# Two token tiles per weight tile: interleaving gate, up, query and value products in two PSUM banks

## Chip, cores, metric

One core of a Trainium2 chip runs the whole program in one launch. The metric is the device time of one execution in microseconds; the time of a kernel is the median of its runs.

## What is computed

A sequence of 256 tokens of width 1024 goes through one mixed block (RWKV-7 time mixing and differential attention side by side, a squared-ReLU feed-forward of width 4096, a gated per-layer embedding), a final norm, and two layers of a second block (SwiGLU feed-forward of width 2816, attention, SwiGLU again). Everything is fp32. The parts that the change touches:

```python
x = x + jnp.square(jax.nn.relu(rmsnorm(x, norm_mlp_g) @ w_ff1)) @ w_ff2
gate = jax.nn.sigmoid(rmsnorm(x, norm_ple_g) @ w_ple_gate)
x = x + (p @ w_ple) * gate
x = rmsnorm(x, final_norm_g)
for layer in range(2):
    x = x + 0.5 * swiglu(rms_norm(x, norm_ffn1), ffn1_w_gate, ffn1_w_up, ffn1_w_down)
    xn = rms_norm(x, norm_mix)
    mixed = (mix_stick_moba, mix_forget_dilated)[layer](xn, w_in, ...)
    x = x + mixed @ w_out
    x = x + 0.5 * swiglu(rms_norm(x, norm_ffn2), ffn2_w_gate, ffn2_w_up, ffn2_w_down)
```

where `swiglu(x, g, u, d) = (silu(x @ g) * (x @ u)) @ d`.

## The kernel before

The 256 tokens are two token tiles t0 and t1 of 128 rows. The residual `x` stays on the chip; the weights (some 252 MB) are streamed through it once. Each weight unit is 128 x 1024 fp32 (512 KB): SP issues its DMA into one of three `raw` buffers (L341), ACT copies it to a rounded `hi` (L365), DVE subtracts to get `lo` (L366), and eleven hi/lo buffers hold the units that TensorE still needs. A product is three matmuls for each row tile of 128 input features (`mm3`): hi weights by hi activations, lo by hi, hi by lo. The weights are the moving operand (128x512), the transposed activations `hT` (for gate, up, queries, values, output) or `aT` (for down) the stationary one. A product of one token tile and 512 output columns is 8 row tiles, 24 matmuls, in one of eight PSUM banks.

The order of TensorE's instructions is written by the program itself, by a planner (`Weave`) that keeps a model time. After each `mm3` it lets side streams run whose due time has passed: the flips (four transposes, an ACT copy `aTh` or `hTh`, a DVE subtraction `aTl` or `hTl`), the attention's own work. The order on the other engines comes from a scheduler. All engines take their instructions in order, so what is listed behind a waiting instruction waits too.

A feed-forward (`mlp`) goes by chunks of 512 (one of 256) hidden columns. For a chunk it takes gate and up for both token tiles (FF1 has one product in place of two). ACT evacuates the first product with the token's norm factor `hT[t].r` (L463), DVE multiplies in the second (L465); this `a` is then flipped. The down product of a chunk (`down`) runs after gate and up of the following chunk; after the last chunk the down products of the last two chunks come in one go, t0 then t1. Its first four row tiles (12 matmuls) need the flip of the chunk before, the next four that of the last chunk.

Order of a chunk before: in the first chunk t0 gate, t0 up, t1 gate, t1 up; later gate t0, gate t1, up t0, up t1. Each is 24 matmuls in a row in one bank.

Attention (`attn_layer`) takes four groups of heads in the order 2, 0, 3, 1; queries and keys of a group are one product of 512 columns, values one of 256 (264 for one of layer 1). Each query product goes to a side stream that normalises, applies rope (L546 to L565; POOL makes one part in the buffer `rb`, of which there is one) and flips. At the end `out` multiplies by `w_out`; its first six row tiles come before the last head group is ready, the last two after. It adds the result to `x` (L876), and the next norm's half begins (`Normed.half`: `h` on DVE L909, a square on ACT L413, a flip). A norm's second half needs the flip of that half only from row tile 4 of the next product on.

`Ple` computes the gated embedding: the gate of t0 (both column halves), the values of t0, the values of t1, the gate of t1.

## Time and profile before

| | |
|---|---|
| median of 3 runs | 1530.09 us (1528.64 to 1535.28) |
| the profiled execution | 1529.78 us |
| its span | 1528.0 us |
| TensorE (PE) busy | 1489.4 us, 97% |
| VectorE (DVE) busy | 927.9 us, 61% |
| ScalarE (ACT) busy | 760.8 us, 50% |
| mean DMA rate | 167 GB/s |

Rough stages: mixed block to 250 us, FF1 to 469, embedding gate to 499, first FFN of layer 0 to 690, attention to 820, second FFN to 1010, and the same three of layer 1 to 1204, 1336 and 1528. A duration of a matmul in the profile overlaps with the next one's; the distance between two starts is what one costs.

### The profile page before, as it was taken

What the parts mean: (1) busy time and instruction counts of PE and PEld (TensorE: products, weight loads), DVE (VectorE), ACT (ScalarE), POOL (GpSimd) and SP (SyncE); (2) the same over time, 40 slices, a digit from 0 to 9 for tenths busy, and PEclk for the clock granted to TensorE, in tenths of its full rate; (3) what the DMA queues carried; (4) which work ended last, traced back from release to release, by engine and by line L of the source; (5) the groups of instructions that cost most, each with busy time, mean ns of one, the idle gap of its engine ahead of it and who ended that gap; (6) DMA issues with size and microseconds to landing.
All of it is one profiled execution on the core that took longest, in us unless ns stands there. A gap on an engine that the chain in (4) does not pass through costs nothing.

```text
span 1528.0 us, 22440 instructions
## 1 busy us (share of the span) xinstructions
PE 1489.4 (97%) x8804; PEld 1237.2 (81%) x8804; DVE 927.9 (61%) x1528; ACT 760.8 (50%) x1142; POOL 46.7 (3%) x70
## 2 busy tenths in 40 slices
PE   7999989999999999999999999999999999999999
PEld 6887767788888788887888888887888888888887
DVE  5886777755558755557546554566545787565552
ACT  6644445644536544447565444445444566464441
POOL 1120100000000000001100000000000010000000
PEclk9999999999999999999999999999999999999999
DMA  7233238655544765536434665547555444275551
GB/s 253 90 118 107 98 119 278 202 194 177 182 151 157 223 200 190 185 132 193 138 111 147 198 194 192 179 156 220 190 189 182 141 154 136 78 227 180 179 182 53
DMA packets 76298, 254.97 MB, mean 167 GB/s; under 512 B 11040, under 2 KB 13344, under 8 KB 76192
## 3 DMA queue, kind: packets, MB, share of 16 engines
q1 hardware_dynamic: 76192, 253.53, 51.1%
q8 instruction: 69, 1.13, 0.3%
q14 instruction: 37, 0.30, 0.1%
HBM read 252.45 MB, written 1.05 MB: 166 GB/s over the span
## 4 chain that ended last, share of the span: by engine, by line
PE 81%; DVE 7%; DMA 5%; ACT 4%; issue 2%; POOL 0%; SPq 0%; ACTq 0%; DVEq 0%; POOLq 0%
PE b L279 77%; DMA raw<-in_w_dram 4%; PE b L283 4%; DVE lo L366 2%; ACT hi L365 2%; DMA grow<-in_norm_mix_g_dram 0%; DMA stage<-in_consts_dram 0%; DMA lam<-in_lam_k_dram 0%; POOL rb L563 0%; POOL rb L562 0%; DVE hTl L366 0%; DVE c L1132 0%; DVE U L1260 0%; DVE u L1129 0%; ACT e L376 0%
## 5 line engine op out<-in xcount | busy, mean ns | idle before, releaser
L366 DVE TENSOR_TENSOR lo<-raw,hi 128x1024 fp32r<-128x1024 f32 (+1 forms) x465 | 561.9, 1214 | 356.1 <-ACT hi L365 350.1
L365 ACT ACTIVATE hi<-raw 128x1024 fp32r<-128x1024 f32 (+1 forms) x465 | 485.6, 1050 | 417.4 <-PE b L279 207.6
L279 PE MATMUL b<-hi,hTh 128*128 128x512 f32 (+2 forms) x1312 | 499.9, 381 | 0.7 <-ACT hi L365 0.7
L279 PE MATMUL b<-hi,hTl 128*128 128x512 f32 (+2 forms) x1312 | 489.9, 373 | 0.5 <-DVE hTl L366 0.5
L279 PE MATMUL b<-lo,hTh 128*128 128x512 f32 (+2 forms) x1312 | 489.7, 373 | 0.8 <-DVE lo L366 0.8
L279 PEld LDWEIGHTS b<-hi,hTl 128*128 128x128 f32 x1312 | 247.4, 189 | 47.8 <-DVE hTl L366 0.9
L279 PEld LDWEIGHTS b<-hi,hTh 128*128 128x128 f32 x1312 | 247.6, 189 | 46.1 <-issue 2.5
L279 PEld LDWEIGHTS b<-lo,hTh 128*128 128x128 f32 x1312 | 247.8, 189 | 44.2 <-DVE lo L366 1.5
L279 PE MATMUL b<-hi,aTh 128*128 128x512 f32 x480 | 191.6, 399 | 0.0
L279 PE MATMUL b<-hi,aTl 128*128 128x512 f32 x480 | 188.1, 392 | 0.0
L279 PE MATMUL b<-lo,aTh 128*128 128x512 f32 x480 | 187.4, 390 | 0.0
L279 PEld LDWEIGHTS b<-hi,aTl 128*128 128x128 f32 x480 | 90.1, 188 | 20.1
L279 PEld LDWEIGHTS b<-lo,aTh 128*128 128x128 f32 x480 | 90.3, 188 | 18.0
L279 PEld LDWEIGHTS b<-hi,aTh 128*128 128x128 f32 x480 | 90.2, 188 | 17.6
L463 ACT ACTIVATE a<-b,rsi_x 128x512 f32<-128x512 f32 (+1 forms) x52 | 34.4, 662 | 55.3 <-PE b L279 55.2
L365 ACT ACTIVATE aTh<-b 128x512 fp32r<-128x512 f32 (+1 forms) x64 | 36.3, 567 | 43.2 <-PE b L283 41.8
L465 DVE SCALAR_TENSOR_TENSOR a<-b,rsi_x,a 128x512 f32<-128x512 f32 (+1 forms) x52 | 37.2, 716 | 32.1 <-PE b L279 17.3
L366 DVE TENSOR_TENSOR aTl<-b,aTh 128x512 fp32r<-128x512 f32 (+1 forms) x64 | 41.8, 653 | 20.0 <-ACT aTh L365 19.7
L279 PE MATMUL b<-hi,hT1h 128*128 128x512 f32 (+1 forms) x128 | 53.4, 418 | 0.0
L279 PE MATMUL b<-lo,hT1h 128*128 128x512 f32 (+1 forms) x128 | 47.8, 373 | 0.6 <-DVE lo L366 0.6
L279 PE MATMUL b<-hi,hT1l 128*128 128x512 f32 (+1 forms) x128 | 47.4, 371 | 0.0
L365 ACT ACTIVATE hTh<-b 128x512 fp32r<-128x512 f32 (+1 forms) x48 | 25.2, 541 | 38.1 <-PE b L283 33.5
(582 smaller groups left out, 1293.6 us busy)
## 6 DMA issues: line engine op xcount, KB each, us to landing
raw<-in_w_dram SPq DMA_DIRECT2D x446, 512.0 KB, 4.2
raw<-in_w_dram SPq DMA_DIRECT2D x16, 384.0 KB, 3.4
grow<-in_norm_ffn_dram SPq DMA_DIRECT2D x4, 512.0 KB, 5.3
x<-in_x_dram SPq DMA_DIRECT2D x4, 256.0 KB, 6.2
x<-in_x_dram SPq DMA_DIRECT2D x2, 512.0 KB, 4.4
grow<-in_norm_mix_dram SPq DMA_DIRECT2D x2, 512.0 KB, 4.8
out_dram<-x SPq DMA_DIRECT2D x4, 256.0 KB, 2.0
raw<-in_w_dram SPq DMA_DIRECT2D x2, 396.0 KB, 3.6
```

What stands on the lines that cost most here:

```text
L279: self.nc.tensor.matmul(out=out, lhsT=lhsT, rhs=rhs, start=start, stop=stop, skip_group_check=skip)
L283: self.nc.tensor.transpose(out=out, in_=src, identity=self.ident)
L365: self.nc.scalar.activation(out=hi, in_=src, func=AF.Copy)
L366: self.nc.vector.tensor_tensor(out=lo, in0=src, in1=hi.bitcast(F32), op=ALU.subtract)
L463: nc.scalar.activation(out=a[t], in_=p, func=AF.Silu if kind == "swiglu" else AF.Relu, scale=hT[t].r)
L465: nc.vector.scalar_tensor_tensor(out=a[t], in0=p, scalar=hT[t].r, in1=a[t], op0=ALU.mult, op1=ALU.mult)
```

## The change

`both` takes a list of weight blocks and, for each, runs both token tiles side by side: for row tile k the three matmuls of t0 into one bank, then the three of t1 into another. Gate and up of each chunk, the values and the queries use it. With `apart` (the first chunk's first product, the first query product) t0 and t1 still run one after the other. In the first chunk the order is then gate t0, gate t1, up of both.

`out` takes both column halves side by side for the first six row tiles, t0 then t1, all before the last head group is waited for, and then the last two row tiles half by half.

In `Ple` the gate's weights come as two blocks of 512 columns, with the value weights between them; the values are copied out of PSUM by ACT (into `pw`, now two buffers), and the products run in the order gate(t0, half 0), values(t0), gate(t1, half 0), gate(t0, half 1), values(t1), gate(t1, half 1).

The number of matmuls, transposes, weight bytes and DMAs is unchanged.

```diff
@@ -451,13 +451,9 @@
         for ci, w in enumerate(chunks):
             kt = w // 128
             ws = [self.wblock((n, i, ci)) for n in names[:-1]]
-            order = [(t, j) for t in range(2) for j in range(nw)] if ci == 0 else [(t, j) for j in range(nw) for t in range(2)]
             a, aT = {}, {}
-            for t, j in order:
-                b = self.bank()
+            for t, j, b in self.both(hT, ws, w, ci == 0):
                 p = b[1][:, :w]
-                for k in range(8):
-                    self.mm3(p, hT[t].at(k), ws[j][k], k == 0, k == 7)
                 if j == 0:
                     a[t] = pool.tile([128, 512], F32, tag="a", name="a", bufs=4)[:, :w]
                     nc.scalar.activation(out=a[t], in_=p, func=AF.Silu if kind == "swiglu" else AF.Relu, scale=hT[t].r)
@@ -474,6 +470,17 @@
                 held = held[1:]
         for t in range(2):
             self.down(acc, t, held, res, after)
+
+    def both(self, hT, ws, n, apart=False):
+
+        for j, w in enumerate(ws):
+            for ts in ((0,), (1,)) if apart and j == 0 else ((0, 1),):
+                bs = [self.bank() for _ in ts]
+                for k in range(8):
+                    for t, b in zip(ts, bs):
+                        self.mm3(b[1][:, :n], hT[t].at(k), w[k], k == 0, k == 7)
+                for t, b in zip(ts, bs):
+                    yield t, j, b
 
     def down(self, acc, t, held, res, after=None):
         fresh = (t, 0) not in acc
@@ -795,10 +802,7 @@
             w = self.wblock((win, 0, ("v", g)))
             n = w[0][0].shape[1]
             vt, bs = [], []
-            for t in range(2):
-                b = self.bank()
-                for k in range(8):
-                    self.mm3(b[1][:, :n], hT[t].at(k), w[k], k == 0, k == 7)
+            for t, _, b in self.both(hT, [w], n):
                 v = pool.tile([128, 256], F32, name="v", tag="v", bufs=5)
                 nc.scalar.activation(out=v, in_=b[1][:, :256], func=AF.Copy, scale=hT[t].r)
                 vt.append(v)
@@ -819,10 +823,7 @@
             else:
                 qkT = [pool.tile([128, 4, 256], F32, name="qkT", tag="qkT", bufs=4)]
             ready = []
-            for t in range(2):
-                b = self.bank()
-                for k in range(8):
-                    self.mm3(b[1], hT[t].at(k), w[k], k == 0, k == 7)
+            for t, _, b in self.both(hT, [w], 512, i == 0):
                 self.held -= 1
                 ready.append(W.spawn(self.qk_side(pool, kind, g, t, b, hT[t], qkT)))
             if i < 3:
@@ -865,29 +866,30 @@
                 self.split(oTs[t][0][:, c], oTs[t][1][:, c], oT[:, c, t * 128:t * 128 + 128])
         acc = {}
 
-        def out(t, s, ks):
-            c = slice(s * 512, s * 512 + 512)
-            if (t, s) not in acc:
-                acc[t, s] = self.bank()
-            p = acc[t, s][1]
+        def out(t, halves, ks):
+            for s in halves:
+                if (t, s) not in acc:
+                    acc[t, s] = self.bank()
             for k in ks:
-                self.mm3(p, (oTs[t][0][:, k], oTs[t][1][:, k]), (wo[k][0][:, c], wo[k][1][:, c]), k == 0, k == 7)
-            if 7 in ks:
+                for s in halves:
+                    c = slice(s * 512, s * 512 + 512)
+                    self.mm3(acc[t, s][1], (oTs[t][0][:, k], oTs[t][1][:, k]), (wo[k][0][:, c], wo[k][1][:, c]), k == 0, k == 7)
+            for s in halves if 7 in ks else ():
+                c = slice(s * 512, s * 512 + 512)
+                p = acc[t, s][1]
                 nc.vector.tensor_tensor(out=self.x[t][:, c], in0=self.x[t][:, c], in1=p, op=ALU.add)
                 self.drop(acc[t, s], 1.0)
                 after(t, s)
 
         first, rest = range(6), range(6, 8)
-        out(0, 0, first)
-        out(0, 1, first)
-        out(1, 0, first)
+        out(0, (0, 1), first)
+        out(1, (0, 1), first)
         W.need(sides[3][0])
-        out(0, 0, rest)
-        out(0, 1, rest)
-        out(1, 1, first)
+        out(0, (0,), rest)
+        out(0, (1,), rest)
         W.need(sides[3][1])
-        out(1, 0, rest)
-        out(1, 1, rest)
+        out(1, (0,), rest)
+        out(1, (1,), rest)
 
 
 GROUPS = (2, 0, 3, 1)
@@ -1041,8 +1043,9 @@
 
 def first_plan():
     out = ffn_plan(("w_ff1", "w_ff2"), 0, FF1_CHUNKS)
-    out.append((("w_ple_gate", 0, 0), (0, D), [(0, D)]))
+    out.append((("w_ple_gate", 0, 0), (0, D), [(0, 512)]))
     out.append((("w_ple", 0, 0), (0, 256), [(0, D)]))
+    out.append((("w_ple_gate", 0, 1), (0, D), [(512, D)]))
     return out
 
 
@@ -1699,42 +1702,53 @@
             lo = pool.tile([128, 2, 128], F32R, name="pTl", tag="pTl", bufs=2)
             self.flips.append(K.flip_side(pt, hi, lo, 4.0))
 
-    def product(self, lhs, w, evacuate):
+    def product(self, lhs, w):
         K = self.K
-        for s in range(2):
-            c = slice(s * 512, s * 512 + 512)
-            b = K.bank()
-            n = len(w)
-            for k in range(n):
-                K.mm3(b[1], lhs(k), (w[k][0][:, c], w[k][1][:, c]), k == 0, k == n - 1)
-            evacuate(s, c, b[1])
-            K.drop(b)
+        b = K.bank()
+        for k in range(len(w)):
+            K.mm3(b[1], lhs(k), w[k], k == 0, k == len(w) - 1)
+        return b
 
     def run(self, pool, hT, after):
         K, nc = self.K, self.K.nc
         K.quota = 4
-        wg = K.wblock(("w_ple_gate", 0, 0))
-        wp = K.wblock(("w_ple", 0, 0))
         gt = [pool.tile([128, D], F32, name="pg", tag="pg", bufs=2) for _ in range(2)]
-        pw = pool.tile([128, D], F32, name="pw", tag="pw", bufs=1)
-
-        def gate(t):
-            self.product(hT[t].at, wg, lambda s, c, p: nc.scalar.activation(out=gt[t][:, c], in_=p, func=AF.Sigmoid, scale=hT[t].r))
-
-        def value(t, evacuate):
+        pw = [pool.tile([128, D], F32, name="pw", tag="pw", bufs=2) for _ in range(2)]
+        half = lambda s: slice(s * 512, s * 512 + 512)
+
+        def gate(t, s, wg):
+            b = self.product(hT[t].at, wg)
+            nc.scalar.activation(out=gt[t][:, half(s)], in_=b[1], func=AF.Sigmoid, scale=hT[t].r)
+            K.drop(b)
+
+        def value(t, s, wp):
             f = K.W.need(self.flips[t])
-            self.product(lambda k: (f[0][:, k], f[1][:, k]), wp, evacuate)
-
-        def merge(t, s, c, v):
-            nc.vector.tensor_tensor(out=gt[t][:, c], in0=gt[t][:, c], in1=v, op=ALU.mult)
+            c = half(s)
+            b = self.product(lambda k: (f[0][:, k], f[1][:, k]), [(h[:, c], l[:, c]) for h, l in wp])
+            nc.scalar.activation(out=pw[t][:, c], in_=b[1], func=AF.Copy)
+            K.drop(b)
+
+        def merge(t, s):
+            c = half(s)
+            nc.vector.tensor_tensor(out=gt[t][:, c], in0=gt[t][:, c], in1=pw[t][:, c], op=ALU.mult)
             nc.vector.tensor_tensor(out=K.x[t][:, c], in0=K.x[t][:, c], in1=gt[t][:, c], op=ALU.add)
             after(t, s)
 
-        gate(0)
-        value(0, lambda s, c, p: merge(0, s, c, p))
-        value(1, lambda s, c, p: nc.scalar.activation(out=pw[:, c], in_=p, func=AF.Copy))
-        self.product(hT[1].at, wg, lambda s, c, p: (
-            nc.scalar.activation(out=gt[1][:, c], in_=p, func=AF.Sigmoid, scale=hT[1].r), merge(1, s, c, pw[:, c])))
+        w = K.wblock(("w_ple_gate", 0, 0))
+        wp = K.wblock(("w_ple", 0, 0))
+        gate(0, 0, w)
+        for s in range(2):
+            value(0, s, wp)
+        merge(0, 0)
+        gate(1, 0, w)
+        w = K.wblock(("w_ple_gate", 0, 1))
+        gate(0, 1, w)
+        merge(0, 1)
+        for s in range(2):
+            value(1, s, wp)
+        merge(1, 0)
+        gate(1, 1, w)
+        merge(1, 1)
 
 
 class FinalNorm(Normed):
```

Three places show how TensorE's order moves (names: `a` the hidden activations of a token tile, `aTh`/`aTl` its flip, `hi`/`lo` weights, `b` a PSUM bank, `h` the scaled input of the next norm; x4 stands for four transposes of one half).

TensorE, last chunk of FF1, before: the transposes of t0's `a` come inside t1's product, those of t1's inside the down product.

```order
L283 MATMUL b_4594<-ident_83,a_4573 128x128 x4
...
L279 MATMUL b_3615<-hi_4465,aTl_4407 128x512
L279 MATMUL b_3615<-hi_4617,aTh_4576 128x512
L279 MATMUL b_3615<-lo_4618,aTh_4576 128x512
L279 MATMUL b_3615<-hi_4617,aTl_4577 128x512
L283 MATMUL b_4654<-ident_83,a_4610 128x128 x4
```

The change, the same place:

```order
L279 MATMUL b_3608<-hi_4458,aTl_4432 128x512
L283 MATMUL b_4644<-ident_83,a_4598 128x128 x4
L283 MATMUL b_4651<-ident_83,a_4603 128x128 x4
L279 MATMUL b_3608<-hi_4610,aTh_4601 128x512
L279 MATMUL b_3608<-lo_4611,aTh_4601 128x512
L279 MATMUL b_3608<-hi_4610,aTl_4602 128x512
```

The 21 matmuls between t0's transposes and the first matmul that reads `aTh` of the last chunk are gone; both tiles' transposes stand right ahead of it. The same is found at the last chunk of all five feed-forwards.

TensorE, end of attention of layer 0 and first gate product of the next FFN, before: t0's `h` (h_7881) is flipped inside the last `out` products, t1's (h_7950) inside t0's gate product, which opens with b_8032.

```order
L283 MATMUL b_7918<-ident_83,h_7881 128x128 x4
...
L283 MATMUL b_7931<-ident_83,h_7881 128x128 x4
...
L279 MATMUL b_7908<-hi_7761,hTl_7768 128x512
L279 MATMUL b_8032<-hi_7986,hTh_7879 128x512
...
L279 MATMUL b_8032<-hi_7992,hTl_7880 128x512
L283 MATMUL b_8042<-ident_83,h_7950 128x128 x4
...
L283 MATMUL b_8055<-ident_83,h_7950 128x128 x4
```

The change, the same place; t0's `h` is h_7903, t1's h_7939, the gate product opens with b_8028:

```order
L283 MATMUL b_7946<-ident_83,h_7903 128x128 x4
...
L279 MATMUL b_7857<-hi_7772,hTl_7779 128x512
L279 MATMUL b_8028<-hi_7982,hTh_7901 128x512
...
L279 MATMUL b_8028<-hi_7982,hTl_7902 128x512
L283 MATMUL b_8032<-ident_83,h_7903 128x128 x4
L283 MATMUL b_8039<-ident_83,h_7939 128x128 x4
...
L279 MATMUL b_8028<-hi_7982,hTl_7902 128x512
L283 MATMUL b_8049<-ident_83,h_7939 128x128 x4
```

Before, 21 matmuls stand between the transposes of t0's first half and the gate's first matmul, and t1's come 9 and 15 matmuls into the gate. Now 3 matmuls stand there, and t0's second half and both halves of t1 are transposed within the gate's first 6 matmuls. Attention of layer 1 ends alike.

TensorE, start of FFN1 of layer 0, before: t0's `a` (a_5266) is flipped 15 matmuls into t1's gate, after gate and up of t0 (48 matmuls).

```order
L279 MATMUL b_5296<-hi_5200,hTh_5060 128x512
L279 MATMUL b_5296<-lo_5201,hTh_5060 128x512
L279 MATMUL b_5296<-hi_5200,hTl_5061 128x512
L283 MATMUL b_5312<-ident_83,a_5266 128x128 x4
L279 MATMUL b_5296<-hi_5200,hTh_5060 128x512
```

The change; t0's `a` is a_5269, t1's a_5296:

```order
L279 MATMUL b_5426<-lo_5387,hTh_4906 128x512
L279 MATMUL b_5426<-hi_5386,hTl_4907 128x512
L283 MATMUL b_5443<-ident_83,a_5269 128x128 x4
L283 MATMUL b_5450<-ident_83,a_5296 128x128 x4
L279 MATMUL b_5427<-hi_5386,hTh_5056 128x512
```

The two flips now come together, 15 matmuls into the second chunk's gate, after gate and up of both tiles (96 matmuls).

## Rows read from the trace of the kernel before

**Rows 1.** The page, busy time by engine: busy us, share of the span, instructions.
```profile
PE 1489.4 (97%) x8804; PEld 1237.2 (81%) x8804; DVE 927.9 (61%) x1528; ACT 760.8 (50%) x1142; POOL 46.7 (3%) x70
```

**Rows 2.** The waits of PE, 240 to 1528 us: engine, line, releaser, total, times, longest.
```profile
PE b L283 <- DVE a L465: 2.7, 3, 2.3
```

**Rows 3.** PE timeline, a gate product: start, duration, engine, line, operation, tiles, idle and releaser.
```profile
407.76 0.40 PE L279 MATMUL b<-hi,hTh 128*128 128x512 f32 x1
...
411.95 0.39 PE L279 MATMUL b<-hi,hTh 128*128 128x512 f32 x1
```

**Rows 4.** PE timeline, a down product, banks alternating every three matmuls.
```profile
425.04 0.39 PE L279 MATMUL b<-hi,aTl 128*128 128x512 f32 x1
...
430.03 0.39 PE L279 MATMUL b<-hi,aTh 128*128 128x512 f32 x1
```

**Rows 5.** Windows: busy us and count by engine, then PEclk, DMA share, GB/s.
```profile
514.40:517.60 3.20, 3.20 (x10) 2.48 (x9) 2.91 (x4) 2.43 (x4) 0.00 (x0) 0.54 0.48 164
905.50:912.50 7.00, 7.00 (x33) 5.75 (x31) 3.12 (x3) 2.62 (x3) 0.00 (x0) 1.00 0.33 114
```

**Rows 6.** PE timeline, start of FFN1 of layer 0.
```profile
510.69 0.40 PE L279 MATMUL b<-hi,hTl 128*128 128x512 f32 x1
513.43 0.66 PE L283 MATMUL b<-ident,a 128*128 128x128 f32 x4 [2.33 <-DVE a L465]
...
514.61 0.59 PE L279 MATMUL b<-hi,hTh 128*128 128x512 f32 x1
...
517.99 0.43 PE L279 MATMUL b<-hi,hTl 128*128 128x512 f32 x1
```

**Rows 7.** PE timeline, second chunk of FFN1 of layer 1.
```profile
1038.43 0.40 PE L279 MATMUL b<-hi,hTl 128*128 128x512 f32 x1
...
1040.74 0.51 PE L279 MATMUL b<-lo,hTh 128*128 128x512 f32 x1 [0.76 <-DVE lo L366]
```

**Rows 8.** PE timeline, attention of layer 0, fourth pair of query products.
```profile
746.45 0.39 PE L279 MATMUL b<-hi,hTl 128*128 128x512 f32 x1
747.84 0.63 PE L283 MATMUL b<-ident,w__7155 128*128 128x128 f32 x4 [1.01 <-DVE w__7155 L565]
```

**Rows 9.** Timeline of all engines, one transposed `a` with nothing in its way.
```profile
1505.22 0.60 PE L283 MATMUL b<-ident,a 128*128 128x128 f32 x4
...
1505.58 0.48 PE L279 MATMUL b<-hi,aTh 128*128 128x512 f32 x1
...
1505.86 0.60 ACT L365 ACTIVATE aTh<-b 128x512 fp32r<-128x512 f32 x1 [5.36 <-PE b L283]
...
1506.49 0.69 DVE L366 TENSOR_TENSOR aTl<-b,aTh 128x512 fp32r<-128x512 f32 x1 [3.74 <-ACT aTh L365]
```

**Rows 10.** The same chain with a weight split ahead on ACT and DVE.
```profile
1183.29 0.60 PE L283 MATMUL b<-ident,a 128*128 128x128 f32 x4
1183.44 1.06 ACT L365 ACTIVATE hi<-raw 128x1024 fp32r<-128x1024 f32 x1 [3.79 <-DMA raw<-in_w_dram]
...
1184.54 1.23 DVE L366 TENSOR_TENSOR lo<-raw,hi 128x1024 fp32r<-128x1024 f32 x1 [2.96 <-ACT hi L365]
...
1185.68 0.68 DVE L366 TENSOR_TENSOR aTl<-b,aTh 128x512 fp32r<-128x512 f32 x1
```

**Rows 11.** Timeline, end of attention of layer 0: DVE and ACT.
```profile
819.89 0.68 DVE L876 TENSOR_TENSOR x<-x,b 128x512 f32<-128x512 f32 x1
...
822.57 0.61 ACT L413 ACTIVATE junk<-x 128x512 f32<-128x512 f32 x1
```

**Rows 12.** ACT timeline, rope of layer 0: the square that opens the chain.
```profile
739.57 0.58 ACT L546 ACTIVATE sq<-b 128x512 f32<-128x512 f32 x1
```

**Rows 13.** POOL timeline, the same chain.
```profile
744.12 1.18 POOL L562 TENSOR_TENSOR rb<-qn,gs 128x256 f32<-128x256 f32 x1 [30.69 <-DVE qn L553]
745.25 1.72 POOL L563 TENSOR_TENSOR rb<-qn,gs 128x256 f32<-128x256 f32 x1
```

**Rows 14.** DVE timeline, the same chain: its end.
```profile
747.00 0.69 DVE L565 TENSOR_TENSOR w__7155<-w__7155,rb 128x512 f32<-128x512 f32 x1 [0.63 <-POOL rb L563]
```

## The prediction

> **What bounds the kernel.** I read the page first: TensorE is busy 97% of the span, no other engine over 61% [rows 1]. Its queue bounds the kernel, so nothing on ACT, DVE or the DMA queues counts before TensorE waits for it. The numbers of matmuls, transposes and weight bytes don't change, so the time can move in three ways only: the distance between two matmuls, TensorE's waits, and its clock. So I next read the waits of PE after 240 us (the mixed block ahead keeps its code) [rows 2], the distances in the PE timelines, and the granted clock.
>
> Distances: 18 steps of a gate product take 411.95 - 407.76 = 4.19 us, 0.233 each [rows 3]; 22 steps of a down product, which alternates between two banks every three matmuls, 430.03 - 425.04 = 4.99, 0.227 each [rows 4]. The granted clock is 1.00 in long matmul runs, which is 2.4 GHz, and 0.54 after the longest wait, near 1.2 GHz [rows 5].
>
> **What it removes.** The waits of before that the new order touches:
>
> 1. Start of FFN1, layer 0. 510.69 to 513.43 is 2.74 us where one step was due: 2.5 lost waiting for t0's `a`, which needs the norm factor of the final norm. Then the clock is down: 514.61 to 517.99 holds 8 steps in 3.38 us, where 8 x 0.233 = 1.86 were due, so 1.5 more [rows 6]. The order now flips `a` after 96 + 15 matmuls in place of 48 + 15, that is 48 x 0.233 = 11 us later; the factor was 2.5 us late. **-4.0**, nothing of it left.
> 2. FFN1, layer 1, second chunk: 1038.43 to 1040.74 is 2.31 us for 2 steps, 1.85 lost on late weights (hi, then lo) [rows 7]. In the first chunk the gate's buffers now come free during t1's gate, 24 matmuls (5.6 us) earlier, and the up weights row by row. **-1.85** (0 if the DMA, not a buffer, was late).
> 3. Attention of layer 0: 746.45 to 747.84, 1.16 lost on the rope of t0's last query product [rows 8]. With both tiles side by side the flip stands about 53 matmuls (12.3 us) behind the pair's end, and the chain takes 8.1 us (below). **-1.16**.
>
> Sum -7.0 us.
>
> **What it adds.** A flip is a chain over three engines. Free of other work: transposes at 1505.22, `aTh` from 1505.86 for 0.60, `aTl` from 1506.49 for 0.69, so 1.96 us until all is there; TensorE itself spends 0.36 on four transposes (1505.22 to the next matmul 1505.58) [rows 9]. With a weight split ahead, 1.06 on ACT and 1.23 on DVE: 1183.29 to 1186.36, 3.07 us [rows 10]. Before, 21 or more matmuls (4.9 us) covered it.
>
> 4. Last chunk of each of five feed-forwards: t0's transposes, t1's, then at once the matmul that reads t0's `aTh`. It could start 0.72 us after the first transposes and gets `aTh` at 1.24: 0.5 lost; the third matmul needs `aTl` at 1.96 where 1.24 + 2 x 0.23 = 1.70 was due: 0.26. So 0.8 each, and 0.8 + 3.07 - 1.96 = 1.9 with a split ahead [rows 9, 10]. FF1's order has two hi copies right ahead of `aTh` and two lo subtractions ahead of `aTl`: 1.7. The last FFN has no weights left: 0.8. The other three, in whose order a single split stands between: 1.0 each, near the free end, since that split has mostly run when the transposes come. **+5.5** (4.0 to 8.4).
> 5. End of both attentions. Set 0 at the end of `out`'s last matmul. t0's first `x` half is final 18 matmuls and four transposes earlier, 18 x 0.233 + 0.36: -4.55. DVE then goes `x` 0.68, lo 1.23, `h`, `x`, `x`, `h` (as large as the first, 0.68 each) [rows 10, 11] to +0.1, a further `h` to 0.8, t1's second `x` to 1.6, lo 1.2 to 2.8, and only then `hTl` of t0's first half, till about 3.6. ACT has, from the second `x` at -1.3, a square 0.6 with its readout 0.2, a hi copy 1.06, t1's square 0.8, then `hTh` 0.6: 2.0. The gate's first matmul was due at 0.2 and starts at about 2.0: 1.8 lost; its third was due at 2.5 and gets `hTl` at about 3.65: 1.15 lost. t0's halves had 21 matmuls of cover before, now 3. **+2.9 per layer, +5.8**. Low end 1.4 per layer (the split of 1.06 to 1.23 not in the way); high end 4.4, with the 1.5 us of clock that the wait of [rows 6] was followed by.
> 6. Rope in attention of layer 1. The chain in layer 0: square at 739.57, rope's end at 747.00 + 0.69, 8.1 us [rows 12, 14]; t1 has to wait for `rb`, which one tile holds from 744.12 to 746.97, 2.9 us [rows 13]. With both tiles ready together t1's is done near 10.5 to 11. In layer 1 the order puts t1's flip about 36 matmuls, 8.5 us, behind the pair. **+2.0** (0 to 3.0).
>
> Within a feed-forward's other chunks the flips stand 15 matmuls (3.5 us) behind the pair, and the second `a` is ready 0.7 later than the first: near 2 us after the pair's end. Nothing. The `Ple` change has the same matmuls; DVE's added halves hide behind 24 matmuls each unless two lo subtractions (2 x 1.23) come first: 0 to +2.5, taken as 0, since the flips' rows keep 12 matmuls ahead. `both` alternates banks as down does [rows 4]: 0.
>
> Sum +13.3; **net +6.3** on the profiled execution's 1529.8 us, 1536.1. That execution is 0.3 under the median, so 1536.4 on the median's scale. Low end of this case -7.0 + 4.0 + 2.8 = -0.2, 1530; high end -7.0 + 8.4 + 8.8 + 3.0 + 2.5 = +15.7, 1546. A measurement here can tell 0.5% (7.7 us) from no change; 1536.4 lies within it.
>
> **The rivals.**
>
> A. The new waits are hidden: the scheduler's order on ACT and DVE is not the one I replayed in time, flips pass ahead, and only the gains are left: -7.0 to 0, 1523 to 1530. For it: the three waits of before are in rows. Against: the 1.96 us of a flip is without any other work, and 3 matmuls (0.7 us) or none can't cover it.
>
> B. The distance of gate and up falls from 0.233 to down's 0.227 when two banks alternate: 2,688 matmuls x 0.006 = -16; with my sum -10, 1520. For it: the two rows differ so. Against: the two rows differ in the stationary tile too (`hTh`, `aTh`), and that stays as it is.
>
> C. Slower: the clock. Each new wait of items 4 and 5 is followed by a drop as at 514.61, 8 steps at 0.42 (+1.5). Seven places: +10.7, so +17, 1547. It decides from the length of the wait: after 2.33 us the clock fell [rows 6], after the 1.16 of [rows 8] the steps went on at full speed. Items 4 are shorter than that; only item 5 comes near.
>
> D. The embedding gate: two lo subtractions ahead of the final norm's `h` take the 2.5 us in full and push the factor of item 1 late again, +2.5 to +5: 1539 to 1541.
>
> E. Alternating banks disturb the clock in every gate and up product. In the rows the granted clock is 1.00 while the down products alternate, at 0.227 a step [rows 4, 5]. If it held for gate and up alone, each of the 51 pairs could lose part of the 1.5 us of [rows 6]; a third of it in each gives +25, with my sum 1562. The Trainium skill's page "TensorE: Matmul & The Clock Gate", section "A second HAM failure mode: psum-queue depth-cycling", says that a kernel that cycled through PSUM banks in each iteration left the engine idle for short moments between groups, and that its clock went back and forth between half and full rate. By that the change would be slower; this case's trace speaks against it, with 1.00 beside alternating banks.
>
> **How the numbers follow.** My case 0.63, A 0.18, B 0.06, C 0.06, D 0.05, E 0.02. The range 1525 to 1546 holds all of my case and D, and two thirds of A; B, C, E and the rest of A are 0.2. Over 0.5% faster is under 1522.4: two thirds of B, and the low end of A with small gains elsewhere, 0.06. Over 0.5% slower is above 1537.7: the upper two fifths of my case (0.24), D, C and E: 0.36. Within: 0.58.
>
> **What would show it.** Right: no wait before a flip of `a` at the start of FFN1 of layer 0; PE waits for ACT `aTh` and DVE `aTl` at the five last chunks, of 0.5 to 1.9 us in all at each; for `hTh` and `hTl` at the first gate of both second FFNs, near 3 us; a wait for rope in layer 1. Steps stay 0.233. Wrong: any of these places without a wait, steps at 0.227, or a granted clock below 1 in feed-forward chunks.

## The result and the profile after

The changed kernel takes 1546.47 us (median of 6 runs, 1538.81 to 1548.00) against 1530.18 for the kernel before (6 runs): ratio 1.0099, 95% interval 1.0083 to 1.0115. The forecast was 1536.4, no difference that can be told, with a range up to 1546. It is slower by 16 us, twice the 7.7 us that the prediction called the least that can be told.

The profiled execution has a span of 1545.3 us, 17.3 more than before. TensorE (PE) is again 97% busy; its busy time rose by 10 us [rows 1] though it has the same matmuls. A busy time that grows at an equal count says that matmuls took longer, so the clock is the next thing to read.

```profile
PE 1499.6 (97%) x8804; PEld 1245.2 (81%) x8804; DVE 923.3 (60%) x1528; ACT 757.3 (49%) x1144; POOL 44.3 (3%) x70
```

Where the time went is best read by stages. The border of a stage is the start of the first matmul that reads `aTh` after one that read `hTh`, or the reverse; such borders exist in every kernel here in the same number (53). The last stage ends at the last matmul. Each column is one profiled execution, in us.

| stage | before | changed | difference |
|---|---|---|---|
| start to first down of FF1 | 304.5 | 303.6 | -1.0 |
| rest of FF1 | 161.5 | 164.0 | +2.5 |
| embedding gate, first two chunks of FFN1, layer 0 | 80.3 | 76.0 | -4.3 |
| rest of FFN1, layer 0 | 143.6 | 146.8 | +3.2 |
| attention of layer 0, first two chunks of FFN2 | 177.2 | 181.4 | +4.2 |
| rest of FFN2, layer 0 | 143.7 | 144.8 | +1.1 |
| first two chunks of FFN1, layer 1 | 48.3 | 46.0 | -2.3 |
| rest of FFN1, layer 1 | 144.7 | 145.8 | +1.1 |
| attention of layer 1, first two chunks of FFN2 | 178.0 | 189.6 | +11.6 |
| rest of FFN2, layer 1 | 142.0 | 143.2 | +1.2 |

The attentions hold most of it, layer 1 far more than layer 0. In the feed-forwards one flip of 0.44 us moves across a border wherever two chunks are interleaved: of the -4.3 and +3.2, and of the -2.3 and +1.1, that much is only moved from one stage to the next.

The waits of PE after 240 us (engine, line, releaser; us in total, times, longest): those for `hTh`, `hTl`, rope (`w`) and `aTh` were forecast, the one for `a` was not; the wait for `a` that before had [rows 2] stood elsewhere, at the start of FFN1 of layer 0.

```profile
PE b L279 <- ACT hTh L365: 3.5, 2, 2.0
...
PE b L279 <- DVE hTl L366: 2.8, 3, 1.0
PE b L283 <- DVE w__11602 L572: 2.1, 1, 2.1
...
PE b L283 <- DVE a L461: 1.5, 1, 1.5
...
PE b L279 <- ACT aTh L365: 1.2, 5, 0.3
```

**End of attention, layer 0.** The PE timeline (start, duration, engine, line, operation, tiles, idle before and what ended it):

```profile
819.96 0.40 PE L279 MATMUL b<-hi,hTl 128*128 128x512 f32 x1
821.89 0.50 PE L279 MATMUL b<-hi,hTh 128*128 128x512 f32 x1 [1.54 <-ACT hTh L365]
822.23 0.40 PE L279 MATMUL b<-lo,hTh 128*128 128x512 f32 x1
823.61 0.50 PE L279 MATMUL b<-hi,hTl 128*128 128x512 f32 x1 [0.98 <-DVE hTl L366]
```

The gate's first matmul was due one step of 0.233 after 819.96 and started at 821.89: 1.70 lost. The third waited for `hTl`: 1.15 lost. In the ACT timeline the `hTh` copy stands behind a weight's hi copy and a square, in the DVE timeline `hTl` behind a lo subtraction:

```profile
819.71 1.04 ACT L365 ACTIVATE hi<-raw 128x1024 fp32r<-128x1024 f32 x1
820.66 0.61 ACT L413 ACTIVATE junk<-x 128x512 f32<-128x512 f32 x1
...
821.27 0.57 ACT L365 ACTIVATE hTh<-b 128x512 fp32r<-128x512 f32 x1
```

```profile
821.61 1.22 DVE L366 TENSOR_TENSOR lo<-raw,hi 128x1024 fp32r<-128x1024 f32 x1
...
822.87 0.69 DVE L366 TENSOR_TENSOR hTl<-b,hTh 128x512 fp32r<-128x512 f32 x1
```

**A last chunk** (FFN1 of layer 1): eight transposes, then 0.25 us of idle for `aTh`, and 0.16 for `aTl` (0.39 from the second matmul to the third, where a step is 0.23). PE timeline:

```profile
1185.78 1.04 PE L283 MATMUL b<-ident,a 128*128 128x128 f32 x8
1187.07 0.50 PE L279 MATMUL b<-hi,aTh 128*128 128x512 f32 x1 [0.25 <-ACT aTh L365]
...
1187.79 0.50 PE L279 MATMUL b<-hi,aTl 128*128 128x512 f32 x1
```

**The rope wait of attention of layer 1**, PE timeline. Two waits stand close together, each ahead of four transposes: 0.92 for t0's rope, 2.05 for t1's. Behind them the steps (from one start to the next) of 128x512 matmuls are 0.57 and 0.43 us in place of 0.31 and 0.23.

```profile
1271.48 0.40 PE L279 MATMUL b<-hi,hTl 128*128 128x512 f32 x1
1272.79 0.66 PE L283 MATMUL b<-ident,w__11582 128*128 128x128 f32 x4 [0.92 <-DVE qn L560]
1275.50 1.12 PE L283 MATMUL b<-ident,w__11602 128*128 128x128 f32 x4 [2.05 <-DVE w__11602 L572]
1276.27 0.78 PE L279 MATMUL b<-hi,hTh 128*128 128x512 f32 x1
1276.84 0.63 PE L279 MATMUL b<-lo,hTh 128*128 128x512 f32 x1
```

What held t1's rope is in the DVE and POOL timelines:

```profile
1270.23 0.69 DVE L572 TENSOR_TENSOR w__11582<-w__11582,rb 128x512 f32<-128x512 f32 x1 [0.71 <-POOL rb L570]
...
1270.92 1.22 DVE L366 TENSOR_TENSOR lo<-raw,hi 128x1024 fp32r<-128x1024 f32 x1
1272.05 0.68 DVE L560 TENSOR_TENSOR qn<-b,rsi_q 128x512 f32<-128x512 f32 x1
```

```profile
1272.88 1.16 POOL L569 TENSOR_TENSOR rb<-qn,gs 128x256 f32<-128x256 f32 x1 [2.68 <-DVE qn L560]
```

The buffer `rb` was free at 1270.92, when t0's last rope step ended. POOL began on t1 only at 1272.88, since t1's `qn` stood on DVE behind that step and behind a lo subtraction.

Windows of the changed kernel (busy us and count of PE, PEld, DVE, ACT, POOL, then PEclk, DMA share, GB/s) show how long half clock lasts behind the waits:

```profile
820.00:830.00 10.00, 7.48 (x31) 5.78 (x30) 9.05 (x28) 5.30 (x10) 0.00 (x0) 0.83 0.52 188
1270.00:1280.00 10.00, 7.03 (x39) 5.10 (x38) 5.51 (x9) 3.14 (x6) 2.04 (x3) 0.74 0.33 111
1280.00:1290.00 10.00, 10.00 (x44) 8.22 (x43) 3.36 (x13) 2.20 (x5) 0.00 (x0) 0.58 0.00 1
1345.00:1355.00 10.00, 7.04 (x32) 5.45 (x31) 9.21 (x28) 6.23 (x12) 0.00 (x0) 0.83 0.48 158
```

The granted clock is 0.74 and then 0.58 over 20 us behind the rope waits, a mix of the full 2.4 and the half 1.2 GHz, and 0.83 over 10 us at each attention's end. Before, a wait of 2.33 was followed by half clock for little more than 3 us [rows 5, 6].

That was not the only drop in the trace of before. In the mixed block, among small products, a wait of 1.70 was followed by steps of 0.22 us between 128x256 matmuls that take 0.12 at full clock, and by half clock for nearly 7 us (its share is 2.8 us of the first window and 4.0 of the second). PE timeline and windows of the kernel before:

```profile
55.93 1.96 PE L279 MATMUL b<-AR,BK 64*128 64x128 f32 x16 [1.70 <-DVE BK L1219]
...
59.80 0.41 PE L279 MATMUL b<-hT1l,hi 128*128 128x256 f32 x1
60.02 0.41 PE L279 MATMUL b<-hT1h,lo 128*128 128x256 f32 x1
```

```profile
50.00:60.00 10.00, 8.30 (x60) 7.82 (x60) 9.84 (x24) 4.42 (x10) 0.96 (x2) 0.86 0.37 114
60.00:70.00 10.00, 10.00 (x72) 9.72 (x70) 7.91 (x18) 4.59 (x8) 1.93 (x5) 0.80 0.13 41
```

**Second chunk of FFN1, layer 0**, a wait that was not forecast. PE waits 1.52 us for `a`; on DVE both tiles' `a` stand behind two lo subtractions:

```profile
546.70 0.39 PE L279 MATMUL b<-hi,aTl 128*128 128x512 f32 x1
548.60 1.32 PE L283 MATMUL b<-ident,a 128*128 128x128 f32 x8 [1.52 <-DVE a L461]
```

```profile
545.35 2.54 DVE L366 TENSOR_TENSOR lo<-raw,hi 128x1024 fp32r<-128x1024 f32 x2 [1.09 <-ACT hi L365]
547.81 1.40 DVE L461 SCALAR_TENSOR_TENSOR a<-b,rsi_g,a 128x512 f32<-128x512 f32 x2
```

### The profile page after: what moved, and what is told of

Same layout as the page of the kernel before. It is cut to its first block, busy times and chain, and to the rows that moved or that the text cites. A ratio compares the mean times of both kernels' runs of the same rounds, so it can differ in the third digit from the quotient of the medians.

```text
span 1545.3 us, 22478 instructions
## 1 busy us (share of the span) xinstructions
PE 1499.6 (97%) x8804; PEld 1245.2 (81%) x8804; DVE 923.3 (60%) x1528; ACT 757.3 (49%) x1144; POOL 44.3 (3%) x70
## 4 chain that ended last, share of the span: by engine, by line
PE 74%; DVE 10%; DMA 7%; ACT 5%; issue 2%; SPq 0%; POOL 0%; POOLq 0%; ACTq 0%; DVEq 0%
PE b L279 71%; DMA raw<-in_w_dram 6%; DVE lo L366 4%; PE b L283 4%; ACT hi L365 3%; DVE hTl L366 0%; DMA x<-in_x_dram 0%; DVE h L911 0%; DMA stage<-in_consts_dram 0%; DMA lam<-in_lam_k_dram 0%; DVE x L880 0%; POOL rb L569 0%; ACT junk L413 0%; DVE U L1263 0%; DVE c L1135 0%
## 5 line engine op out<-in xcount | busy, mean ns | idle before, releaser
L365 ACT ACTIVATE aTh<-b 128x512 fp32r<-128x512 f32 (+1 forms) x64 | 33.1, 566 | 53.6 <-PE b L283 53.4
L366 DVE TENSOR_TENSOR hTl<-b,hTh 128x512 fp32r<-128x512 f32 (+1 forms) x48 | 29.2, 619 | 27.9 <-ACT hTh L365 27.9
```

The costliest lines, as they stand in the source:

```text
L365: self.nc.scalar.activation(out=hi, in_=src, func=AF.Copy)
L366: self.nc.vector.tensor_tensor(out=lo, in0=src, in1=hi.bitcast(F32), op=ALU.subtract)
```

## The experiments

Theory after the result (called clock theory in the expectations): the waits are about those forecast, and the surplus is half clock behind three of them. The rival (bank theory): two banks in turn cost time in every interleaved product.

**Queries undone.**

```diff
-            for t, _, b in self.both(hT, [w], 512, i == 0):
+            for t, _, b in self.both(hT, [w], 512, True):
```

> The changed kernel with its query products one token tile after the other again (all four head groups, both layers); all else as changed. Clock theory: the changed kernel loses 3.3 us to two rope waits in attention of layer 1 (before: 1.3 us at that place) and then 6.8 us to a granted clock of half rate over some 13 us behind them; both go (-8.8), and the rope wait of attention of layer 0 comes back (+1.2): about 7.6 us under the changed kernel, near 1539 us. Bank theory (two banks in turn cost time in every product): 16 of some 140 interleaved products change, so less than 2 us.

Measured: 1545.22 us, ratio to before 1.0093 (1.0077 to 1.0108). A miss: some 1 us in place of 7.6. The granted clock does come back (1.00 over 1260 to 1290, and 0.993 to 0.995 over the whole execution in the six runs, where the changed kernel mostly had 0.989 to 0.990), and the stage of attention of layer 1 falls from 189.6 to 184.8. But other waits grew or came new. PE timeline, two rows of FFN1 of layer 0 and one of attention of layer 1:

```profile
549.21 1.97 PE L283 MATMUL b<-ident,a 128*128 128x128 f32 x8 [3.49 <-DVE a L461]
...
551.41 0.63 PE L279 MATMUL b<-lo,aTh 128*128 128x512 f32 x1
...
1319.79 0.50 PE L279 MATMUL b<-hi,hTh 128*128 128x512 f32 x1 [2.36 <-ACT hTh L365]
```

At 1319.79 the output product's first matmul waits 2.36 us for `hTh`, a wait that neither kernel had. At 549.21 the unforecast wait of the second chunk is 3.49 where it was 1.52, with a clock drop behind it (0.42 steps), and that stage takes 151.1 us in place of 146.8, though all engines' orders are the same up to there. That wait differs between executions: five kernels have the same orders up to there (the changed one, queries undone, output product undone, waits filled, queries and values undone), and their profiled executions have 1.52, 3.49, 4.41, 3.37 and 2.83. It goes with when weights land, as far as the queues were followed. A stage of one execution is uncertain by so much, and the median of a kernel's runs decides.

**Output product undone** (`out` one column half after the other, as in the kernel before):

```diff
-        out(0, (0, 1), first)
-        out(1, (0, 1), first)
+        out(0, 0, first)
+        out(0, 1, first)
+        out(1, 0, first)
         W.need(sides[3][0])
...
+        out(1, 1, first)
```

> The changed kernel with the output product of attention in its old order (one column half after the other, the second half of t1 as cover for t0's flips). Clock theory: the waits for hTh and hTl at the first gate product go, 2.8 us in layer 0 and 3.3 in layer 1, and the half clock behind each (1.7 us each): about 9.5 us under the changed kernel, near 1537 us. If only the waits count and the clock does not follow them: 6 us. Bank theory: no more than 1 us, since the last two row tiles already went half by half.

Measured: 1535.94 us, 1.0037 (1.0023 to 1.0050), 9.5 us less by the ratios, as expected. The waits for `hTh` and `hTl` are gone in both layers, and the stages fall by 5.1 and 9.3 us, while the wait near 545 us and the clock behind it take 4.0 more in this execution. Not all of the 9.3 belongs to the edit: the rope waits are there unchanged (0.90 and 2.05), but in this execution the clock behind them came back sooner. Windows of this kernel:

```profile
1270.00:1280.00 10.00, 7.05 (x44) 5.37 (x42) 5.70 (x16) 3.41 (x8) 1.84 (x2) 0.83 0.32 106
1280.00:1290.00 10.00, 10.00 (x64) 7.93 (x63) 6.37 (x23) 4.73 (x10) 0.00 (x0) 1.00 0.15 54
```

So the same pair of waits is followed by a long stretch of half clock in one execution and a short one in another.

**Last chunks undone** (`both` with gate and up apart at the last chunk):

```diff
-            for t, j, b in self.both(hT, ws, w, ci == 0):
+            for t, j, b in self.both(hT, ws, w, range(nw) if ci == len(chunks) - 1 else (0,) if ci == 0 else ()):
```

> The changed kernel with the last chunk of each of the five feed-forwards in its old order (gate t0, gate t1, up t0, up t1, one bank at a time). The waits for aTh and aTl go: 1.2 us in FF1, 0.6 in each of the other four, 3.7 us in all, and the clock was not down behind them: near 1543 us. Bank theory: 9 of some 140 interleaved products change, 1 us of 16.

Measured: 1540.11 us, 1.0058 (1.0036 to 1.0080), 6.3 us less by the ratios. No last chunk waits for `aTh` or `aTl` any more. The stages that hold little else (rest of FF1, rest of both FFN2) are 1.3, 0.8 and 0.8 shorter. Another 2.1 came from attention of layer 0, which the edit does not touch: in this execution the clock did not fall behind the same two waits (1.75 and 1.10).

**All three undone.** The three edits together.

> The changed kernel with all three undone at once: queries, output product and last chunks in the old order; the other chunks, the values and the embedding gate stay interleaved. Clock theory: 7.6 + 9.5 + 3.7 = 20.8 us under the changed kernel, near 1526 us, some 4 us under the kernel before, since the early FFN waits stay away. Bank theory: most of the loss stays, over 1535 us.

Measured: 1532.74 us, 1.0011 (0.9996 to 1.0025). Most of the loss is gone, so the bank theory's "over 1535" fails, but 13.5 us came back by the ratios where 20.8 were expected (the three edits alone gave 0.9, 9.5 and 6.3, together 16.7): the wait of 2.36 us ahead of the output product of layer 1 is here too, and one of 1.3 for a `v` copy in layer 0.

**The waits filled.** Nothing is undone; matmuls without use keep TensorE busy through three waits.

```diff
+        if kind == "dilated" and g == 3 and t == 1:
+            for _ in range(8):
+                nc.tensor.matmul(out=tb[1], lhsT=hT.dst[0][:, 0], rhs=hT.dst[0][:, 0:4], start=True, stop=True, skip_group_check=True)
...
+                if fill and j == 0 and ts[0] == 0:
+                    for _ in range(fill):
+                        self.nc.tensor.matmul(out=bs[0][1], lhsT=w[0][0][:, 0:128], rhs=w[0][0], start=True, stop=True, skip_group_check=True)
```

> The changed kernel, nothing taken away, with matmuls added whose result is overwritten: 8 of 128x512 between the two rope transposes of the late wait in attention of layer 1, and 8 ahead of the first gate product of both second FFNs. They fit into the waits (8 x 0.21 = 1.7 us) and keep TensorE busy there; what the waits wait for comes no earlier. Clock theory: the 10 us that half clock costs behind the three waits (6.8 + 1.7 + 1.7) go, the waits themselves stay: near 1537 us, with a granted clock near 1.00 over 820 to 830, 1270 to 1290 and 1340 to 1360. If the waits alone (or the banks) set the time: no change from 1546, or slightly slower.

Measured: 1538.66 us, 1.0060 (1.0038 to 1.0082), 6 us less by the ratios and 7.8 by the medians. This is the run that separates clock from wait: more work, the same waits, less time. The granted clock of its six executions is 0.993 to 0.998, where five of the six of the changed kernel have 0.989 or 0.990; the means differ by 0.0055, and that share of 1546 us, 8.5 us, is an estimate of what the clock gives back (half clock lowers the mean by half its share of the time, and half of its time is lost). Windows at the three places, and the PE timeline of the rope wait:

```profile
825.00:835.00 10.00, 9.02 (x47) 7.07 (x46) 10.00 (x31) 6.50 (x14) 0.00 (x0) 1.00 0.61 217
1276.00:1286.00 10.00, 8.85 (x62) 6.92 (x61) 6.97 (x19) 4.13 (x9) 1.88 (x2) 1.00 0.31 106
1286.00:1296.00 10.00, 10.00 (x62) 7.88 (x61) 6.19 (x22) 5.10 (x10) 0.00 (x0) 1.00 0.16 54
1343.00:1353.00 10.00, 8.81 (x46) 6.64 (x45) 10.00 (x28) 7.47 (x15) 0.00 (x0) 1.00 0.39 136
```

```profile
1278.30 0.66 PE L283 MATMUL b<-ident,w__11590 128*128 128x128 f32 x4 [0.90 <-DVE qn L563]
1278.71 2.08 PE L646 MATMUL b<-hTh 128*128 128x512 f32 x8
1281.05 0.66 PE L283 MATMUL b<-ident,w__11610 128*128 128x128 f32 x4 [0.25 <-DVE w__11610 L575]
```

The clock is 1.00 everywhere there. t1's transposes still start 2.75 us after t0's (2.71 in the changed kernel), so the wait itself has not moved. From them the next 140 PE instructions take 21.3 us, where the same ones take 27.3 in the changed kernel: half clock at this place costs 6.0 us. From the gate's third matmul at the two attention ends 30 PE instructions take 5.6 us in place of 7.2 and 7.1: 1.6 and 1.5.

Two limits. This profiled execution is the slowest of the six, 1545.42 us: the stages of the two attentions are 1.1 and 7.0 shorter than the changed kernel's, but the rest of FFN1 of layer 0 is 4.3 longer, with a wait of 3.37 near 552 us and a clock of 0.66 over 550 to 560. And full clock behind a wait can come unfilled too, as at the end of attention of layer 0 with last chunks undone. So the profile shows what half clock costs at each place; that filling removes it more often than not rests on the six times and clocks.

**Attention as before, last chunks as before** (the other chunks and the embedding gate as changed). Against all three undone only the values differ; that part of the edit:

```diff
-            for t, _, b in self.both(hT, [w], n):
+            for t in range(2):
+                b = self.bank()
+                for k in range(8):
+                    self.mm3(b[1][:, :n], hT[t].at(k), w[k], k == 0, k == 7)
```

> Attention wholly as before (values too) and last chunks as before; the other feed-forward chunks interleaved and the new embedding gate. Theory: with values interleaved the last v of t0 comes 24 matmuls later, and the wait of 2.6 us for hTh ahead of the output product of layer 1 is its price, with 1 us more behind the v copy in layer 0; both go here: some 3.5 us under the kernel with three parts undone, near 1529 us. Rival: that wait belongs to the last head group's softmax whatever the values do, then it stays, near 1532.5 us.

Measured: 1528.35 us, 0.9989 (0.9975 to 1.0003). The wait ahead of the output product is gone, as is that behind the `v` copy. The values are the only difference, so their interleaving is what these two waits come from; the changed kernel has its values interleaved too and shows neither wait; that TensorE comes there later in it is the likely reason, not shown.

**Inner chunks alone, and the embedding gate alone**, each added to the kernel before.

> The kernel before with feed-forward chunks interleaved except the last of each; embedding gate and attention as before. Theory: the wait at the start of FFN1 of layer 0 shrinks from 2.5 us (plus 1.5 of clock) and the late weights of layer 1 go (1.85): 2 to 5 us under the kernel before, 1525 to 1528 us. Bank theory: 5 to 10 us slower than before.

> The kernel before with the new embedding gate alone. The same matmuls and bytes; the factor of the final norm comes when it came or somewhat later: 0 to 2 us slower than before, 1529 to 1532 us. If the new gate were a part of the loss of its own: 4 us or more.

Measured: 1528.66 us, 0.9988 (0.9974 to 1.0003), and 1529.63, 0.9997 (0.9981 to 1.0012). Neither can be told from no change, and interleaving by itself costs nothing that shows: the bank theory is out. The first gains 4.4 and 2.4 us in the two stages that hold first chunks and gives back 3.5 in the rest of FFN1 of layer 0 and 2.1 in FF1. With the gate alone the wait for `a` at the start of FFN1 grew from 2.33 to 3.09.

**The order of the first chunk alone.**

```diff
-            order = [(t, j) for t in range(2) for j in range(nw)] if ci == 0 else [(t, j) for j in range(nw) for t in range(2)]
+            order = [(t, j) for j in range(nw) for t in range(2)]
```

> The kernel before with one edit: in the first chunk of each feed-forward the products go gate t0, gate t1, up t0, up t1, as in all later chunks. No product is interleaved, attention and embedding gate are as before. Theory: what the change gains comes from this order alone. t0's first flip stands 24 matmuls (5.6 us) later, so the wait for the final norm's factor (2.5 us and 1.5 of clock) goes, and the gate's buffers come free 24 matmuls earlier, so the late weights of layer 1 go (1.85); the wait that the interleaved second chunk has at about 545 us (1.5 to 4.4 us) stays away, since there t0's flip stands 24 matmuls ahead of t1's: 4 to 5 us under the kernel before. Rival: weights are late at that stretch in any order, and the wait moves to another place: no difference from before.

> The kernel before with the first chunk of each feed-forward as the change has it (gate t0, gate t1, up of both side by side) and all later chunks in the old order. Theory: the same gains as the edit of order alone, 4 to 5 us under the kernel before, and no wait near 545 us. If interleaving itself cost or gave something, this kernel and the one with the order alone would differ by more than 2 us.

Measured: 1527.76 us, 0.9978 (0.9967 to 0.9989), and 1526.97, 0.9978 (0.9968 to 0.9988): 3.4 us under the kernel before, the two alike. These are faster than either kernel of the case. What was expected at the places came only in part. With the order alone the wait for `a` at the start of FFN1 is 1.18 where it was 2.33, with no half clock behind it, and late weights still cost 0.76 in layer 1. With the pair that wait is gone, but two waits of 0.76 for weights stand in its place. The wait near 545 us, which was to stay away, is there too. PE timeline with the pair:

```profile
546.64 0.39 PE L279 MATMUL b<-hi,aTl 128*128 128x512 f32 x1
548.03 0.66 PE L283 MATMUL b<-ident,a 128*128 128x128 f32 x4 [1.00 <-DVE a L461]
```

It is 1.00 here (0.88 with the order alone), where the kernels with an interleaved second chunk have 1.02 (all three undone) to 4.41; the kernel before has none. Where the 3.4 us lie is not shown: from the first down product of FF1 on the profiled executions take 1223.5 us (order alone), 1222.5 (pair) and 1223.5 (before), and ahead of it, where all three have the same orders, they differ by 1.9.

**Queries and values undone.**

> The changed kernel with query and value products one token tile after the other; output product, feed-forwards and embedding gate as changed. Theory: with queries alone undone the waits moved to the output product of layer 1 (2.6 us) and behind a v copy in layer 0 (1.5 us); with values undone as well both go: 3 to 4 us under the kernel with queries undone (1545), near 1541 us. Rival: those waits come from the output product's new order; then it stays at 1545.

Measured: 1545.44 us, 1.0089 (1.0066 to 1.0112). A miss. The wait ahead of the output product is gone, and the stage of attention of layer 1 by a further 2.1 us to 182.7, so the rival fails at that place. But attention of layer 0 took 183.3, with a granted clock of 0.76 and 0.90 in the 20 us behind its end: one wait less, and the clock lost more behind another that was left. Its six runs go from 1536.36 us, with a clock of 0.996, to 1548.64, with 0.992.

## Why the prediction was wrong, point by point

- **Item 1, -4.0:** right at its place: -4.3 by the stage table, -3.9 without the flip that only moved. But "Within a feed-forward's other chunks ... Nothing" failed. In the second chunk both `a` come at the pair's end, DVE has two lo subtractions ahead, weights land late in that stretch, and the flips stand 15 matmuls behind: 1.67 us in the changed kernel's profile, up to 4.6 in others. The stage after lost 3.2, of which 2.0 here and 0.8 at its last chunk.
- **Item 2, -1.85, and item 3, -1.16:** right. The stage of the late weights is 2.3 shorter, 1.9 without the moved flip, and no rope wait stands in the changed kernel's fourth pair of layer 0.
- **Item 4, +5.5:** place and mechanism right, the size near the low end of 4.0 to 8.4. The waits are 0.46 and 0.77 in FF1 and 0.46 and 0.15 in each of the other four. With the longer step behind each wait, from the transposes to the seventh matmul behind them, FF1 lost 1.4 and the others 0.8 each against the same stretch without a wait: 4.5. The four have the same 0.25 of idle for `aTh`, the last FFN's, with no weights left, among them: no split stood in the way, and the free chain's 0.8 was the right one.
- **Item 5, +5.8:** right, 2.85 and 3.28 us, released by the engines and in the order worked out. The 1.5 us of clock of its high end came at both ends (1.6, 1.5), while the sum carried none.
- **Item 6, +2.0:** the size of the wait was right, 1.08 + 2.26 against 1.31 of before ahead of the product of `qkT` there, but partly by luck: t1 did not wait for the one buffer `rb`, which was free in time, but for its `qn` behind other work on DVE. **The step that failed is its price.** The sum took the wait alone, and rival C said that the clock "decides from the length of the wait" and that "only item 5 comes near". A wait of 0.92 and, four transposes later, one of 2.05 brought half clock for 13 us, 6.0 us of cost, four times the 1.5 that was read from the drop of [rows 5, 6]. The trace of before could have warned: the prediction read its waits from 240 us on, and at 55.93 us a shorter wait, 1.70, was followed by half clock for twice as long.

Two merged flips cost no more than two apart. From the first transpose to the third matmul behind it, eight transposes take 377.77 - 376.44 = 1.33 us, four take 1506.13 - 1505.22 = 0.91. Less two steps of 0.23 that is 0.87 for two flips in one, and 2 x 0.45 for two apart. PE timeline of the changed kernel, and one row of the kernel before that goes with [rows 9]:

```profile
376.44 1.04 PE L283 MATMUL b<-ident,a 128*128 128x128 f32 x8
...
377.77 0.40 PE L279 MATMUL b<-hi,aTl 128*128 128x512 f32 x1
```

```profile
1506.13 0.40 PE L279 MATMUL b<-hi,aTl 128*128 128x512 f32 x1
```

Sum with measured sizes: -3.9 - 1.9 - 1.2 + 4.5 + 6.1 + 2.0 = +5.6 for the items, where +6.3 was forecast. Clock behind items 5 and 6, put at nothing in the sum: +9.1. The second chunk: +2.0. Together 16.7 of the 17.3 us of the profiled execution. The clock is more than half of it. One of the six runs took 1538.81 us, with a clock of 0.995 in place of 0.989: near the forecast, which had the waits without the clock.

Two slips of arithmetic change nothing: the chances of over 0.5% slower add up to 0.37, not 0.36, and rival B's 2,688 matmuls count the five first products that stay apart; the 51 pairs are 2,448, some -15 us.

**Rivals.** A fell: each place that was named has its wait. B and E fell: the steps of gate and up stay at a median of 0.232 us, the granted clock of the changed kernel is 1.00 in every interleaved product of its feed-forwards (only the two gate products right behind the waits of item 5, which are not interleaved, have less), and the kernel with nothing but inner chunks interleaved is no slower. The rule cited under E (the Trainium skill, "TensorE: Matmul & The Clock Gate", "A second HAM failure mode: psum-queue depth-cycling") is not borne out by these runs. C was the right mechanism, and its 1547 is close to the measured 1546.47 by luck: it put 1.5 us on each of seven places, while no window's clock is lowered at the five of item 4, and the rope wait, which it did not name, cost 6.0. D: the gate alone takes no longer than before (0.9997), though the factor of item 1 came some 0.8 later there. Of the signs of being wrong, one came, a granted clock below 1 in a feed-forward chunk: the first gate product of both second FFNs (0.83 over 10 us).

What stays open: why the same waits are followed by half clock for 3 us in one execution and 13 in another, or by none (the attention end in layer 0 with last chunks undone). The wait near 545 us was only followed to DVE's queue and late weights; no run took either away. That the second chunk's interleaving makes it longer is argued: the kernels without it have 0.88 and 1.00, one with it has 1.02.

## What to carry to other kernels

A wait on TensorE's path has two prices: its own length and that of the clock behind it, which in one sparse stretch (attention with small products) was nearly twice the wait, and in some executions nothing. To tell them apart, fill the wait with matmuls without use and see whether the time falls. And look for the part of an interleaving that pays: here the only kernels clear of the one before were the two that change nothing but the first chunk (0.9978), while the last chunks, the output product, the queries and the values, where interleaving left too little other work to cover what follows a product, gave back more than was gained.

## What the runs showed of the hardware that was not expected

Half clock after a wait lasted over 13 us at one place (1275.5 to 1288.6, 140 instructions in 27.3 us for 21.3), nearly 7 at another (before, behind the wait of 1.70 at 55.93) and little more than 3 at others. Behind some waits it came in one execution and not in another. The spread of a kernel's runs (1538.81 to 1548.00 for the changed one) goes with the granted clock, 0.995 to 0.989.
